# The state-space tables of a two-layer block, made in steps of four groups instead of two

## The chip, the cores and the metric

The kernel runs on one core of one Trainium2 chip. The metric is the device time of one execution in microseconds (us). Three runs of the kernel before gave 1955.3, 1954.03 and 1954.87 us, so the median is 1954.87 us. One execution was recorded by the profiler; its own time is 1953.94 us and its span, from the first to the last instruction, is 1951.7 us.

## The reference, cut to what matters

The reference is a two-layer block that works on 512 latent tokens and 256 context tokens of width 1024, in float32. Each layer normalises and modulates its input, projects it into four groups of heads (A: a gating MLP, B: a chunked linear attention, C: the state-space mixer S5, D: latent attention), joins them by an output projection, and then runs a gated MLP with a short convolution over its rows.

What the change touches is a part of group C. In the reference it reads:

```python
lam_bar = jnp.exp(lam * dt)
b_bar = ((lam_bar - 1.0) / lam)[..., None] * b
...
bu = jnp.einsum('bngi,gpi->bngp', u.astype(jnp.complex64), b_bar)
a = jnp.broadcast_to(lam_bar, bu.shape)
a_cum, h = lax.associative_scan(_linear_recurrence, (a, bu), axis=1)
...
ys_x.append(f(jnp.einsum('bngp,gop->bngo', hx, cmat).real))
```

There are 16 groups of 16 channels, 64 complex states in each, and two directions (the second runs over the flipped sequence).

## The kernel before, in words

**How the scan is tiled.** The kernel does not scan token by token. It cuts the sequence into chunks of 8 tokens. For each layer and each direction it prepares four tables from the parameters alone: `E` (how the 8 tokens of a chunk enter the state), `G` (how the state at a chunk's start reaches its 8 outputs), `K` (how tokens of one chunk reach one another) and `L` (the powers of lambda over whole chunks). The function `s5_tables` (from L446) makes them and stores them to DRAM; `mixer_c` (from L642) loads them and uses them.

**What a table step does.** After a prefix (exponentials, sine and cosine, powers of lambda up to 8, L453 to L530) and a set-up for each direction (L564 to L588), the groups are worked off in steps of two, so there are 8 steps in a direction and 16 in a layer. One step has six VectorE (DVE) operations: L600 and L601 multiply, L602 adds (128 x 288 elements each, the tile `gt`), and L623, L624, L625 do the same for the tile `et` (128 x 256 each). SyncE (SP) stores `gt` as `G` (L606). TensorE (PE) makes two small matmuls for `K` (L610) and two transposes of `et` (L627), all of them into one PSUM bank `kp`: columns 0 to 127 take the `K` part and columns 128 to 383 the transposes. ScalarE (ACT) copies the transposes to `es` (L629, 128 x 256), from where SP stores them as `E` (L630), and copies 64 rows of the `K` part to `ks` (L632). After the last step of a direction, `ks` is corrected (L634 or L636) and stored in four DMAs (L639).

**Buffers.** `gt`, `gt2` (the second product) and `et` have two buffers each, `es` and `ks` one. The PSUM tag is `pb1` in the first layer and `pn` in the second; both have two banks. The ten small tiles of the prefix (`are`, `aim`, `ldt`, `dt`, `mag`, `zr`, `zi`, `kk`, `sn`, `cs`) have a place of their own.

**When the steps are issued.** `s5_tables` is a generator, and a `yield` stands ahead of each step. For the first layer the prefix is traced at the start of the program; all the rest is traced at the beginning of `mixers`, after the opening stage, in which x is normalised and modulated (`nsa` L310, `nu` L388, `hh` L389, `hl` L390; the reciprocal root is taken on DVE in a chain of tiny operations, L132 to L138) and the first projection runs (`pm`). For the second layer it is traced inside the up-projection of the first layer's MLP: each call of `ffn_up` with c == 0 is followed by four `next(tables)`. One such call makes two products of 24 matmuls for 512 columns and 24 for 256 (`pf`, L198 to L200); their PSUM tiles are freed by ACT (L1196) and by DVE (L1198), which apply the convolution, and the weights are split into two parts by ACT (`whi`, L190) and DVE (`wlo`, L191).

**What sets the order.** The framework fixes the order of the instructions of each engine when the program is built. It simulates the program, prefers what was traced earlier, and lets later work fill the gaps that it foresees. At run time each engine works its queue off in that order: an instruction that waits holds back all that stands behind it on its engine. SP issues every DMA of the kernel, in order as well.

Of the kernel before, what the change touches and what calls it, by code (L numbers as in the profile page):

```python
# [15 lines left out]
ALU = mybir.AluOpType  # L16
# [73 lines left out]
class Net:  # L90
# [352 lines left out]
    def s5_tables(self, l, p, psp, p1):  # L443


        nc, tc = self.nc, self.tc  # L446
        tt, ts, stt = nc.vector.tensor_tensor, nc.vector.tensor_scalar, nc.vector.scalar_tensor_tensor
        n = 32

        def tl(tag, shape=(128, n)):  # L450
            return self.t(p, shape, tag)

        are, aim, ldt = tl("are"), tl("aim"), tl("ldt")  # L453
        self.load_sm(l, "are", are[:])
        self.load_sm(l, "aim", aim[:])
        self.load_sm(l, "ldt", ldt[:])
        dt, mag, zr, zi = tl("dt"), tl("mag"), tl("zr"), tl("zi")
# [4 lines left out]
        kk, sn, cs = tl("kk"), tl("sn"), tl("cs")  # L462
        ts(kk[:], zi[:], 0.15915494309189535, 12582912.0, op0=ALU.mult, op1=ALU.add)
# [16 lines left out]
        for d in range(2):  # L480
# [5 lines left out]
            m = 1  # L486
# [13 lines left out]

        fr, fi, dn, t1 = tl("ek"), tl("er"), tl("eq"), tl("kk")
        nr = tl("zr")
        for d in range(2):
# [15 lines left out]
        ev = self.s5d[l]  # L519
# [8 lines left out]

        early = [ld(x, 1, y) for x, y in (("bre", "bx"), ("bim", "by"), ("cx", "cx"), ("cy", "cy"))]
        yield  # L530

        cp = self.t(p, [128, 2, 128], "es", bufs=1)[:].rearrange("p r (m g) -> p r m g", m=8)
        for gh in range(2):
# [27 lines left out]
        for d in (1, 0):  # L561
# [5 lines left out]
            nc.vector.tensor_copy(eb[hi], pw[hi, 0, d])  # L567
            bre, bim, cx, cy = early if d else [ld(x, 0, y) for x, y in (
                ("bre", "bx"), ("bim", "by"), ("cx", "cx"), ("cy", "cy"))]
# [3 lines left out]
            b1 = self.t(p, [128, 2, 9, 16], "gt2", bufs=2)[:].rearrange("p a b c -> p (a b c)")[:, :256].rearrange(  # L573
                "p (a b) -> p a b", b=16)
# [13 lines left out]
            nc.vector.tensor_copy(bb[hi, :256], bbi[hi].rearrange("p a b -> p (a b)"))  # L588
            for g0 in range(0, 16, 2):
                yield  # L590
                gs = slice(g0, g0 + 2)

                sh = [128, 2, 9, 16]
                gt = self.t(p, sh, "gt", bufs=2)
                g2 = self.t(p, sh, "gt2", bufs=2)

                def co(c):
                    return c[:, :, gs].rearrange("p j g -> p g j").unsqueeze(3).to_broadcast(sh)

                tt(gt[:], cx[:, gs, :].unsqueeze(2).to_broadcast(sh), co(ea), op=ALU.mult)  # L600
                tt(g2[:], cy[:, gs, :].unsqueeze(2).to_broadcast(sh), co(eb), op=ALU.mult)  # L601
                tt(gt[:], gt[:], g2[:], op=ALU.add)  # L602
                jo, ko = 1 - d, d
                kp = self.t(psp, [128, 512], p1)[:]
                pe = kp[:, 128:384]
                nc.sync.dma_start(ev["G"][:, d, gs, :],  # L606
                                  gt[:, :, jo:jo + 8, :].rearrange("p g j o -> p g (j o)"))
                for g in range(g0, g0 + 2):
                    q = g % 4
                    nc.tensor.matmul(kp[32 * q:32 * q + 32, 0:128],  # L610
                                     bb[:, g * 16:g * 16 + 32],
                                     gt[:, g - g0, ko:ko + 8, :].rearrange("p j o -> p (j o)"),
                                     start=True, stop=True)

                sh2 = [128, 2, 8, 16]
                et = self.t(p, sh2, "et", bufs=2)
                e2 = self.t(p, sh, "gt2", bufs=2)[:].rearrange("p a b c -> p (a b c)")[:, :256].rearrange(
                    "p (g s i) -> p g s i", g=2, s=8)
# [674 lines left out]
    def run(self, out):  # L1293
# [76 lines left out]
        for l in range(L):  # L1370
# [4 lines left out]
            with self.pool("f") as fp, self.pool("psf", space=PSUM) as psp:  # L1375
# [43 lines left out]
                with ExitStack() as ye:  # L1419
# [368 lines left out]
```

## Time and profile before

| what | value |
|---|---|
| median of three runs | 1954.87 us (1954.03 to 1955.3) |
| profiled execution, its own time | 1953.94 us |
| its span | 1951.7 us |
| PE busy | 1793.4 us (92%) |
| DVE busy | 1201.3 us (62%) |
| ACT busy | 784.5 us (40%) |
| mean granted TensorE clock | 0.931 of full speed |
| chain that ended last: PE, DVE, issue, ACT | 68%, 15%, 10%, 4% |

"Busy" is the time in which an engine has at least one instruction running. The chain that ended last is followed back from the last instruction, at each step to what released it. Idle time of an engine that is not on that chain costs nothing. The duration of a DVE row is longer than the distance to the next row, because neighbours overlap a little; the distance from start to start is what a queue full of work pays.

### The profile page before, as it was taken

What the parts mean: (1) busy time and instruction counts of PE and PEld (TensorE: products, weight loads), DVE (VectorE), ACT (ScalarE), POOL (GpSimd) and SP (SyncE); (2) the same over time, 40 slices, a digit from 0 to 9 for tenths busy, and PEclk for the clock granted to TensorE, in tenths of its full rate; (3) what the DMA queues carried; (4) which work ended last, traced back from release to release, by engine and by line L of the source; (5) the groups of instructions that cost most, each with busy time, mean ns of one, the idle gap of its engine ahead of it and who ended that gap; (6) DMA issues with size and microseconds to landing.
All of it is one profiled execution on the core that took longest, in us unless ns stands there. A gap on an engine that the chain in (4) does not pass through costs nothing.

```text
span 1951.7 us, 28485 instructions
## 1 busy us (share of the span) xinstructions
PE 1793.4 (92%) x11256; PEld 1535.1 (79%) x11256; DVE 1201.3 (62%) x2296; ACT 784.5 (40%) x1284; POOL 124.1 (6%) x142
## 2 busy tenths in 40 slices
PE   5799999789989899999999987997979999999997
PEld 2577687569987688888888886986668988888886
DVE  8938644555788963674575575684465666364646
ACT  3332744245763333332331354355434554343432
POOL 0000000000340000000000034000000130000002
PEclk7699998779999999999999987998788989999998
DMA  9374621002633333443344243322100722323241
GB/s 352 99 253 168 209 85 42 28 25 101 216 110 107 112 106 108 124 138 117 123 130 136 66 146 105 115 75 86 42 23 23 238 78 84 109 86 108 87 132 63
DMA packets 96949, 222.18 MB, mean 114 GB/s; under 512 B 11440, under 2 KB 45616, under 8 KB 95792
## 3 DMA queue, kind: packets, MB, share of 16 engines
q1 hardware_dynamic: 96816, 220.36, 35.3%
q8 instruction: 89, 1.46, 0.3%
q14 instruction: 44, 0.36, 0.1%
HBM read 193.35 MB, written 24.08 MB: 111 GB/s over the span
## 4 chain that ended last, share of the span: by engine, by line
PE 68%; DVE 15%; issue 10%; ACT 4%; DMA 2%; POOL 1%; SPq 1%; POOLq 0%; DVEq 0%; ACTq 0%
PE pf L198 15%; PE pf L199 15%; PE pf L200 15%; PE pg L198 3%; PE pg L200 3%; PE pg L199 3%; DVE wlo L191 1%; PE pd L1142 1%; DVE z L1198 1%; PE pb L242 1%; DVE nu L388 1%; PE pn L321 1%; PE pc L767 1%; DVE junk L235 1%; DVE hlx L390 1%
## 5 line engine op out<-in xcount | busy, mean ns | idle before, releaser
L191 DVE TENSOR_TENSOR wlo<-raw,whi 128x1024 fp32r<-128x1024 f32 (+1 forms) x215 | 252.4, 1174 | 306.4 <-ACT whi L190 303.4
L190 ACT ACTIVATE whi<-raw 128x1024 fp32r<-128x1024 f32 (+1 forms) x215 | 217.4, 1011 | 403.0 <-PE pf L199 326.7
L198 PE MATMUL pf<-hhx,whi 128*128 128x512 f32 (+1 forms) x1032 | 364.8, 359 | 15.1 <-DVE z L1198 8.8
L199 PE MATMUL pf<-hlx,whi 128*128 128x512 f32 (+1 forms) x1032 | 367.9, 358 | 6.1 <-DVE hlx L390 5.9
L200 PE MATMUL pf<-hhx,wlo 128*128 128x512 f32 (+1 forms) x1032 | 366.5, 356 | 2.0 <-DVE wlo L191 1.8
L198 PEld LDWEIGHTS pf<-hhx,whi 128*128 128x128 f32 x1032 | 198.7, 195 | 43.4 <-ACT hhx L389 5.6
L199 PEld LDWEIGHTS pf<-hlx,whi 128*128 128x128 f32 x1032 | 201.0, 195 | 33.5 <-DVE hlx L390 8.8
L200 PEld LDWEIGHTS pf<-hhx,wlo 128*128 128x128 f32 x1032 | 200.9, 195 | 28.8 <-DVE wlo L191 3.0
L198 PE MATMUL pf<-g,whi 128*128 128x512 f32 (+1 forms) x552 | 185.0, 341 | 5.8 <-DVE z L1198 3.1
L200 PE MATMUL pf<-g,wlo 128*128 128x512 f32 (+1 forms) x552 | 186.4, 340 | 0.8 <-DVE wlo L191 0.8
L199 PE MATMUL pf<-g,whi 128*128 128x512 f32 (+1 forms) x552 | 186.9, 340 | 0.0
L1198 DVE SCALAR_TENSOR_TENSOR z<-pf,cols,z 128x511 f32<-128x511 f32 (+1 forms) x264 | 168.3, 655 | 24.2 <-ACT z L1196 21.8
L199 PE MATMUL pf<-hl,whi 128*128 128x256 f32 x432 | 123.5, 287 | 0.5 <-DVE hl L390 0.5
L198 PE MATMUL pf<-hh,whi 128*128 128x256 f32 x432 | 122.0, 287 | 1.6 <-ACT hh L389 1.5
L200 PE MATMUL pf<-hh,wlo 128*128 128x256 f32 x432 | 122.6, 285 | 0.0
L198 PEld LDWEIGHTS pf<-g,whi 128*128 128x128 f32 x552 | 104.2, 191 | 19.2 <-issue 3.9
L200 PEld LDWEIGHTS pf<-g,wlo 128*128 128x128 f32 x552 | 105.2, 191 | 12.3 <-DVE wlo L191 1.0
L199 PEld LDWEIGHTS pf<-g,whi 128*128 128x128 f32 x552 | 105.3, 191 | 11.6 <-DVE g L1248 0.2
L1196 ACT ACTIVATE z<-pf,cols 128x512 f32<-128x512 f32 (+1 forms) x132 | 90.0, 696 | 33.9 <-PE pf L200 29.3
L1277 DVE TENSOR_TENSOR y<-y,pf 128x512 f32<-128x512 f32 (+1 forms) x88 | 44.2, 513 | 72.4 <-PE pf L200 72.3
L124 POOL TENSOR_TENSOR nroy<-nroy,mhalf 128x2 f32<-128x2 f32 x10 | 10.0, 996 | 1232.4 <-DVE nroy L123 900.7
L198 PEld LDWEIGHTS pf<-hh,whi 128*128 128x128 f32 x432 | 83.0, 194 | 3.7 <-ACT hh L389 2.1
(467 smaller groups left out, 3489.4 us busy)
## 6 DMA issues: line engine op xcount, KB each, us to landing
raw<-in_w SPq DMA_DIRECT2D x170, 512.0 KB, 3.5
rawm<-in_wmod SPq DMA_DIRECT2D x64, 512.0 KB, 4.2
raw<-in_w SPq DMA_DIRECT2D x48, 384.0 KB, 3.1
wm<-in_wmod SPq DMA_DIRECT2D x8, 1024.0 KB, 11.1
silu<-in_wmod SPq DMA_DIRECT2D x16, 512.0 KB, 5.5
dx<-g SPq DMA_DIRECT2D x32, 256.0 KB, 2.2
dG<-gt SPq DMA_DIRECT2D x32, 128.0 KB, 1.9
dE<-es SPq DMA_DIRECT2D x32, 128.0 KB, 1.8
```

What stands on the lines that cost most here:

```text
L190: nc.scalar.activation(hv, src, AF.Copy)
L191: nc.vector.tensor_tensor(lv, src, hv.bitcast(F32), op=ALU.subtract)
L198: self.nc.tensor.matmul(out, lh, rh, start=i == 0, stop=False)
L199: self.nc.tensor.matmul(out, lh, rl, start=False, stop=False)
L200: self.nc.tensor.matmul(out, ll, rh, start=False, stop=i == n - 1)
L235: self.nc.vector.scalar_tensor_tensor(junk[:], wt, 1.0, self.silu[w][:], op0=ALU.mult, op1=ALU.mult, accum_out=self.modacc[l][:, w, m:m + 1])
L242: self.nc.tensor.matmul(acc[32 * q:32 * q + 2, :], self.ct[:, k, :], halves[q // 2][:, q % 2 * 512:q % 2 * 512 + 512], start=k == 0, stop= ...
L321: self.nc.tensor.matmul(ps[:, j:j + 1], acc[:, k, j * 128:(j + 1) * 128], self.ones[:, 0:1], start=k == 0, stop=k == 1)
L388: nc.vector.scalar_tensor_tensor(u[:], xk, sc, pb, op0=ALU.mult, op1=ALU.mult)
L1196: nc.scalar.activation(z[:, o:o + m], p[:, :m], AF.Identity, bias=b, scale=w1)
L1198: self.last = nc.vector.scalar_tensor_tensor(z[:, o + d:o + d + m - 1], p[:, s:s + m - 1], w, z[:, o + d:o + d + m - 1], op0=ALU.mult, op1 ...
L1277: nc.vector.tensor_tensor(y[:, m, t0:t0 + tw], y[:, m, t0:t0 + tw], ps[:, :tw], op=ALU.add)
```

## The change

The groups of a direction are worked off in four steps of four groups. Each of the six DVE operations of a step is twice as wide (128 x 576 and 128 x 512 elements). One PSUM bank `kp` is taken at the first step of a direction and holds the `K` parts of all four steps; `ks` is copied from it once, after the last step. The four transposes of a step go into another bank `pe`, taken at each step. `gt` keeps two buffers of double size; `gt2` and `et` have one buffer of double size each, `es` stays at one, of double size. The ten small tiles of the prefix are moved into the tile that is later used for `ks`. In the up-projection each `ffn_up` call with c == 0 is followed by two `next(tables)` instead of four. There are now 10 pieces of the generator instead of 18: the first call takes the prefix and the first set-up, the next four calls take two steps each (with the second set-up in the third call). Before, the first call took two steps of two groups as well, the next three calls had four each, and the fifth had the last two.

```diff
+        def four(tag, j=9):
+            return self.t(p, [128, 4, 9, 16], tag, bufs=2 if tag == "gt" else 1)[:, :, :j]
+        early = tl("ks", (128, 4, 128))[:].rearrange("p a b -> p (a b)")
+        small = {}
+        def sm(tag):
+            return small.setdefault(tag, early[:, len(small) * n:len(small) * n + n])
...
-            for g0 in range(0, 16, 2):
+            kp = None
+            for g0 in range(0, 16, 4):
                 yield
-                gs = slice(g0, g0 + 2)
-                sh = [128, 2, 9, 16]
-                gt = self.t(p, sh, "gt", bufs=2)
-                g2 = self.t(p, sh, "gt2", bufs=2)
+                if kp is None:
+                    kp = self.t(psp, [128, 512], p1)
+                gs = slice(g0, g0 + 4)
+                sh = [128, 4, 9, 16]
+                gt, g2 = four("gt"), four("gt2")
...
-                kp = self.t(psp, [128, 512], p1)[:]
-                pe = kp[:, 128:384]
...
-                for g in range(g0, g0 + 2):
-                    q = g % 4
-                    nc.tensor.matmul(kp[32 * q:32 * q + 32, 0:128],
+                for q in range(4):
+                    nc.tensor.matmul(kp[32 * q:32 * q + 32, g0 * 32:g0 * 32 + 128],
...
-                et = self.t(p, sh2, "et", bufs=2)
+                et = self.t(p, sh2, "et", bufs=1)
+                e2 = four("gt2", 8)
...
+                pe = self.t(psp, [128, 512], p1)
-                for g in range(2):
+                for g in range(4):
                     nc.tensor.transpose(pe[:, g * 128:g * 128 + 128], ...)
-                es = self.t(p, [128, 2, 128], "es", bufs=1)
-                nc.scalar.copy(es[:].rearrange("p g c -> p (g c)"), pe)
-                nc.sync.dma_start(ev["E"][:, d, g0:g0 + 2, :], es[:])
-                rs = slice(g0 % 4 * 32, g0 % 4 * 32 + 64)
-                nc.scalar.copy(ks[rs, g0 // 4, :], kp[rs, 0:128])
+                es = self.t(p, [128, 4, 128], "es", bufs=1)
+                nc.scalar.copy(es[:].rearrange("p g c -> p (g c)"), pe[:])
+                nc.sync.dma_start(ev["E"][:, d, gs, :], es[:])
+            nc.scalar.copy(ks[:].rearrange("p a b -> p (a b)"), kp[:])
...
                             if c == 0:
-                                for _ in range(4):
+                                for _ in range(2):
                                     next(tables, None)
```

## Rows read from the trace of the kernel before

**Rows 1.** The page, the span in 40 slices of 48.8 us, tenths busy.
```profile
PE   5799999789989899999999987997979999999997
DVE  8938644555788963674575575684465666364646
```

**Rows 2.** Stretches: busy us of each engine (instructions), granted clock, DMA share, GB/s.
```profile
48.00:62.00 14.00, 10.45 (x69) 7.07 (x68) 14.00 (x47) 5.64 (x17) 0.00 (x0) 0.80 0.51 175
62.00:77.00 15.00, 9.80 (x38) 6.98 (x38) 14.70 (x51) 5.02 (x12) 0.88 (x2) 0.50 0.27 77
...
98.00:110.00 12.00, 10.11 (x56) 7.36 (x53) 4.43 (x9) 6.51 (x14) 0.00 (x0) 0.86 0.73 256
...
632.00:658.00 26.00, 21.08 (x128) 16.76 (x127) 25.31 (x62) 9.14 (x18) 0.00 (x0) 1.00 0.47 139
701.00:720.00 19.00, 17.98 (x99) 15.51 (x98) 11.36 (x18) 8.14 (x12) 0.00 (x0) 1.00 0.37 117
```

**Rows 3.** DVE's instructions in order, 47 to 62 us: start, duration, line, tiles.
```profile
48.73 0.16 DVE L133 TENSOR_SCALAR nri<-nrx 128x2 int32<-128x2 int32 x1
...
53.07 0.15 DVE L137 TENSOR_TENSOR nrt<-nrt,nri 128x2 f32<-128x2 f32 x1
53.14 0.41 DVE L625 TENSOR_TENSOR et<-et,gt 128x256 f32<-128x256 f32 x1
53.48 0.42 DVE L623 TENSOR_TENSOR et<-bbr,ea 128x256 f32<-128x256 f32 x1
53.81 0.45 DVE L602 TENSOR_TENSOR gt<-gt,gt 128x288 f32<-128x288 f32 x1
54.18 0.15 DVE L138 SCALAR_TENSOR_TENSOR nry<-nrt,nri 128x2 f32<-128x2 f32 x1
...
59.97 0.15 DVE L138 SCALAR_TENSOR_TENSOR nry<-nrt,nry 128x2 f32<-128x2 f32 x1
```

**Rows 4.** DVE's instructions in order, for distances from start to start.
```profile
23.73 0.44 DVE L600 TENSOR_TENSOR gt<-cx,ea 128x288 f32<-128x288 f32 x1
24.10 0.41 DVE L623 TENSOR_TENSOR et<-bbr,ea 128x256 f32<-128x256 f32 x1
24.43 0.44 DVE L601 TENSOR_TENSOR gt<-cy,eb 128x288 f32<-128x288 f32 x1
...
27.98 0.67 DVE L310 TENSOR_TENSOR nsa<-nsa,nsq 128x512 f32<-128x512 f32 x1
28.58 0.41 DVE L623 TENSOR_TENSOR et<-bbr,ea 128x256 f32<-128x256 f32 x1
...
81.62 0.42 DVE L623 TENSOR_TENSOR et<-bbr,ea 128x256 f32<-128x256 f32 x1 [0.94 <-PE pb L627]
82.08 0.42 DVE L625 TENSOR_TENSOR et<-et,gt 128x256 f32<-128x256 f32 x1
```

**Rows 5.** ACT's instructions in order: the copies, and one wait.
```profile
97.41 0.37 ACT L629 COPY es<-pb 128x256 f32<-128x256 f32 x1 [3.04 <-PE pb L627]
97.81 0.26 ACT L632 COPY ks<-pb 64x128 f32<-64x128 f32 x1
...
101.95 0.58 ACT L676 COPY s5a<-pc 96x512 f32<-96x512 f32 x1 [1.18 <-PE pc L675]
...
696.42 1.06 ACT L190 ACTIVATE whi<-raw 128x1024 fp32r<-128x1024 f32 x1 [7.40 <-PE pf L199]
...
697.84 0.36 ACT L629 COPY es<-pn 128x256 f32<-128x256 f32 x1
```

**Rows 6.** Who waited for whom, 0 to 110, then 590 to 700: total us, times, longest.
```profile
ACT es L629 <- DMA dE<-es: 12.0, 6, 3.9
...
ACT es L629 <- DMA dE<-es: 11.1, 6, 2.4
PE pf L198 <- DVE z L1198: 8.8, 5, 2.5
DVE et L623 <- PE pn L627: 3.4, 1, 3.4
```

More of the change, by code (lines that the diff above doesn't have):

```diff
@@ L451, in tl @@
             return self.t(p, shape, tag)
-        are, aim, ldt = tl("are"), tl("aim"), tl("ldt")
+        def four(tag, j=9):
[4 more added lines that the diff above has]
+            return small.setdefault(tag, early[:, len(small) * n:len(small) * n + n])
+        are, aim, ldt = sm("are"), sm("aim"), sm("ldt")
         self.load_sm(l, "are", are[:])
@@ L499, in s5_tables @@
                 m *= 2
-        fr, fi, dn, t1 = tl("ek"), tl("er"), tl("eq"), tl("kk")
-        nr = tl("zr")
+        fr, fi, dn, t1 = tl("ek"), tl("er"), tl("eq"), sm("kk")
+        nr = sm("zr")
         for d in range(2):
@@ L527, in ld @@
             return dst
-        early = [ld(x, 1, y) for x, y in (("bre", "bx"), ("bim", "by"), ("cx", "cx"), ("cy", "cy"))]
+        first = [ld(x, 1, y) for x, y in (("bre", "bx"), ("bim", "by"), ("cx", "cx"), ("cy", "cy"))]
         yield
-        cp = self.t(p, [128, 2, 128], "es", bufs=1)[:].rearrange("p r (m g) -> p r m g", m=8)
+        cp = self.t(p, [128, 4, 128], "es", bufs=1)[:, :2].rearrange("p r (m g) -> p r m g", m=8)
         for gh in range(2):
@@ L567, in s5_tables @@
             nc.vector.tensor_copy(eb[hi], pw[hi, 0, d])
-            bre, bim, cx, cy = early if d else [ld(x, 0, y) for x, y in (
+            bre, bim, cx, cy = first if d else [ld(x, 0, y) for x, y in (
                 ("bre", "bx"), ("bim", "by"), ("cx", "cx"), ("cy", "cy"))]
@@ L572, in s5_tables @@
             fib = fi[:, d * 16:d * 16 + 16].unsqueeze(2).to_broadcast([128, 16, 16])
-            b1 = self.t(p, [128, 2, 9, 16], "gt2", bufs=2)[:].rearrange("p a b c -> p (a b c)")[:, :256].rearrange(
+            b1 = self.t(p, [128, 4, 9, 16], "gt2", bufs=1)[:].rearrange("p a b c -> p (a b c)")[:, :256].rearrange(
                 "p (a b) -> p a b", b=16)
@@ L597, in co @@
                 def co(c):
                     return c[:, :, gs].rearrange("p j g -> p g j").unsqueeze(3).to_broadcast(sh)
-                tt(gt[:], cx[:, gs, :].unsqueeze(2).to_broadcast(sh), co(ea), op=ALU.mult)
-                tt(g2[:], cy[:, gs, :].unsqueeze(2).to_broadcast(sh), co(eb), op=ALU.mult)
-                tt(gt[:], gt[:], g2[:], op=ALU.add)
+                tt(gt, cx[:, gs, :].unsqueeze(2).to_broadcast(sh), co(ea), op=ALU.mult)
+                tt(g2, cy[:, gs, :].unsqueeze(2).to_broadcast(sh), co(eb), op=ALU.mult)
@@ L603, in s5_tables @@
+                tt(gt, gt, g2, op=ALU.add)
                 jo, ko = 1 - d, d
-                kp = self.t(psp, [128, 512], p1)[:]
-                pe = kp[:, 128:384]
                 nc.sync.dma_start(ev["G"][:, d, gs, :],
                                   gt[:, :, jo:jo + 8, :].rearrange("p g j o -> p g (j o)"))
-                for g in range(g0, g0 + 2):
-                    q = g % 4
-                    nc.tensor.matmul(kp[32 * q:32 * q + 32, 0:128],
-                                     bb[:, g * 16:g * 16 + 32],
-                                     gt[:, g - g0, ko:ko + 8, :].rearrange("p j o -> p (j o)"),
+                for q in range(4):
+                    nc.tensor.matmul(kp[32 * q:32 * q + 32, g0 * 32:g0 * 32 + 128],
+                                     bb[:, (g0 + q) * 16:(g0 + q) * 16 + 32],
+                                     gt[:, q, ko:ko + 8, :].rearrange("p j o -> p (j o)"),
@@ L613, in s5_tables @@
                                      start=True, stop=True)
-                sh2 = [128, 2, 8, 16]
-                et = self.t(p, sh2, "et", bufs=2)
-                e2 = self.t(p, sh, "gt2", bufs=2)[:].rearrange("p a b c -> p (a b c)")[:, :256].rearrange(
-                    "p (g s i) -> p g s i", g=2, s=8)
+                sh2 = [128, 4, 8, 16]
+                et = self.t(p, sh2, "et", bufs=1)
+                e2 = four("gt2", 8)
                 def ce(c):
```

4 lines of the change are left out of this document (2 added, 2 removed).

## The prediction, made before the change was run

> **What bounds the kernel now.** I went from the slices to the stretches, then to single instructions. In the slices PE is busy nine tenths or more nearly everywhere, and where it is not, DVE is high [rows 1]. The two dips that concern us are the first two slices (PE 5 and 7, DVE 8 and 9) and the slices around 590 to 690 us (DVE 8 and 9 again). These are the two places where the state-space tables are made. A change to the tables can move the end only there, or through what they hand on.
>
> The stretches say how tight it is [rows 2]. From 48 to 62 us DVE is busy 14.00 of 14 us, from 62 to 77 us 14.70 of 15, while PE has 10.45 and 9.80 us of work at a granted clock of 0.80 and 0.50, so part of the time it was at its 1.2 GHz level. After 98 us DVE falls to 4.43 of 12 us and PE takes over. In the second layer's tables one call of the up-projection (632 to 658 us) has DVE at 25.31 of 26 us. The call from 701 to 720 us has DVE at 11.36 of 19 and PE at 17.98 of 19: there PE is the bound, and DVE work is free.
>
> Why DVE decides, and not only by its total, is seen in its order of instructions [rows 3]. The reciprocal root for the second token group is a chain of two-element operations, the second of them at 48.73, the last at 59.97 us. Between two neighbours of that chain, 53.07 and 54.18, three table operations stand in the queue. The chain waits for no one; it goes slowly because table work is queued between its links. So the tables lie on the opening path although the opening needs none of them.
>
> **The change, part by part.**
>
> *DVE operations.* Distances from start to start count, since the queue is full [rows 4]: 0.37 us for 128 x 288 (23.73 to 24.10), 0.33 for 128 x 256 (24.10 to 24.43), 0.60 for 128 x 512 (27.98 to 28.58). For 128 x 576 I extrapolate: 0.60 + 64 x (0.60 - 0.37)/224 = 0.67 us, an estimate. Two old steps cost 6 x 0.37 + 6 x 0.33 = 4.20 us; a new one 3 x 0.67 + 3 x 0.60 = 3.81. That saves 0.4 us for each of 8 new steps in a layer, 3.2 us a layer, 6.4 in all.
>
> Here a rule of the Trainium skill would give more. The rows show the next operation starting 0.37 us after one whose own duration is 0.44 [rows 4]. The page "VectorE: DVE Perf Modes", section "The DRAIN you can't avoid", says that the next op does not start until the pipe has emptied, which would make the duration the price: 12 durations of 0.44 and 0.41 against 6 of 0.74 and 0.67 save 0.88 us a step, 14 us in all instead of 6.4. The trace disagrees with that rule as it stands there (the same page allows that an op which is not held starts earlier), and I go by the distances.
>
> *Lost interleaving.* `gt2` and `et` go from two buffers to one. Now the operations of two steps can stand alternately; afterwards `gt2` forces second product, sum, next second product, sum to follow one another. An operation right behind its own producer started 0.46 us after it instead of 0.33 (81.62 to 82.08) [rows 4]: 0.13 us for each such pair. Three pairs in a step would cost 0.39 x 8 = 3.1 us a layer, none costs 0. I take one in a step, since the first product of the next step and the free `et` product can stand between: 1.0 us. Net for DVE: -2.2 us a layer, between -3.2 and -0.1.
>
> *What of it is on the path.* In the first layer DVE is full from 48 us to the end of the opening, so I count all of -2.2. In the second layer the five calls alternate between a full DVE and a full PE [rows 2], so I count -1.5 of -2.2 (ends: 0 and -3.2).
>
> *The step that moves.* With two pieces a call instead of four, four groups (3.8 us of DVE) go from the first call to the fifth, which is bounded by PE and has 7.6 us of DVE time free. The ends are 0 and -3.8. Since the planner pulls table work forward into gaps anyway, the place of the `next` decides little; I take -0.8.
>
> *ACT.* Old: 16 x (0.37 + 0.26) = 10.1 us a layer for the copies of `es` and `ks`. New: 8 + 2 copies of 512 columns at 0.58 (the row of 96 x 512) = 5.8 us [rows 5]. The 4.3 us saved lie on an engine that is idle more than half of the time (5.64 of 14, 9.14 of 26) [rows 2], so they are worth nothing by themselves. But `es` has one buffer, and its copy waited 12.0 and 11.1 us in the two stages for the store of the copy before [rows 6], holding back whatever stood behind it on ACT, the weight splits and the convolution's first pass among it. Eight copies instead of sixteen, one every 3.8 us or more of DVE work, meet that wait seldom. I take -0.5 (ends 0 and -2).
>
> *PE, SP, prefix.* PE makes the same 64 small matmuls and 32 transposes a layer; nothing. SP issues 8 stores fewer of `G` and of `E` each per layer, and none is on the path that I can show; nothing, at most a gain for the loads behind them. `ks` is copied once at the end instead of bit by bit, so the last four stores of a direction come one 0.58 us copy later, where PE has other work (10.11 of 12 us after 98 us) [rows 2]. The small tiles share a place with `ks`, whose next writer is DVE too: nothing.
>
> *Sum.* -2.2 (first layer) - 1.5 (second) - 0.8 (moved step) - 0.5 (ACT) = -5.0 us. The profiled execution took 1953.94 us, 2.2 us more than its span, and becomes 1948.9; the median of the runs is 0.93 us higher, so 1949.9 us. The favourable ends together give -3.2 - 3.2 - 3.8 - 2 = -12.2 us, which is 1942.7; the unfavourable ones leave nothing.
>
> **The rivals.**
>
> *The path loses the tables (faster by more).* With one buffer of `gt2` and `et`, fewer table operations are ready at a time. If the planner then puts one long operation between two links of the root's chain instead of two or three short ones, each link shrinks from about 1.1 to 0.7 us. With nine links from 48.73 to 59.97 that is 3.6 us more, and the same holds for the convolution's passes in the second layer. The work left out goes to where PE is the bound. Against it: nothing in the rows says how the order will come out. Time: 1943.
>
> *The long operations fill as much (no change).* If two of them stand between two links, that is 1.27 us instead of 1.04, 0.23 x 9 = 2 us more in this chain and about as much in the chain for the third token group behind it. From -5.0 some -1 is left: 1953.9 us, no difference.
>
> *The single buffers stall PE and DVE (slower).* A step's transposes now need the one free PSUM bank, so they wait for the `es` copy of the step before, and the next `et` product waits for the transposes. That copy stands in ACT's queue behind a weight split, which once waited 7.40 us for PE itself [rows 5]. With two half-size buffers, DVE already waited once 3.4 us for PE to finish its transposes, and PE waited up to 2.5 us for DVE [rows 6]. It decides from where a step's copy ends later than the next step's `et` sum, 3.8 us of DVE work on. If 3 or 4 of the 16 new steps are caught for 2.5 to 3.4 us, that costs about 10 us and leaves +5: 1960 us. What is queued behind the waiting transposes is the whole up-projection. For it: PE works its queue in order and has no slack there. Against it: there are half as many meeting points, and ACT is seldom behind by that much. The Trainium skill has the rule that speaks for this rival: "Double-buffer for performance", on the page "Trainium Kernel Development and Optimization", section "Best Practices". The row of 3.4 us agrees that a buffer can run out here; how often with one buffer no row of before can show.
>
> **How the numbers follow.** Forecast 0.45 (its own range 1946 to 1952.5), larger gain 0.12, no change 0.23, slower 0.20. A measurement of this kernel tells 0.2% (3.9 us) from no change, so faster means below 1951.0 and slower above 1958.8. Of the forecast 0.36 lies below 1951.0; with the larger gain that is 0.48. The rest of the forecast and nearly all of the third case make 0.31, the last case and a tail of the third 0.21. The range from 1942 to 1959 leaves out about half of the largest gains and half of the stalls, 0.16 together.
>
> **What would show it.** Right: table operations of DVE at distances of 0.60 and 0.67 us; DVE busy time lower by some 5 us over the two stages; the waits of `es` for its own store down from 23 us to a few; the last matmul of the opening projection 2 us earlier; calls of the up-projection around 600 to 700 us shorter by 2 to 3 us together, with more DVE work in the fifth. Wrong: waits of PE for `es` or of DVE for transposes that add up to more than 5 us; a root's chain longer than the 11.2 us of now; or a gain that lies outside 0 to 110 and 580 to 720 us, which none of my steps would explain.

## The result

The changed kernel took 1929.91 us in the median (1923.23 to 1937.35 us, four runs) against 1954.77 us for the kernel before (1954.03 to 1955.3, four runs): a ratio of 0.9874 with a 95% interval of 0.9832 to 0.9916. In a second series it was 0.9873 (0.9858 to 0.9888). The gain is 25 us; the forecast was 5, and the lower end of its range 1942. The profiled execution took 1925.66 us, its span is 1923.6 us.

From the page of the changed kernel, the span in 40 slices, tenths busy and tenths of the full clock [rows 1]:

```profile
PE   4799999789989899999999988997988999999997
DVE  8938544555789952764675585684564675454645
PEclk8799998689999999999999986997998999999998
```

The clock row of the kernel before, which the prediction did not use:

```profile
PEclk7699998779999999999999987998788989999998
```

The tables are made in the first two slices and in the 13th to 15th. Both rows also dip around the eighth slice and from the 24th on, where the mixers and the latent attentions of the two layers stand, and they differ there as well. The prediction did not look at these slices.

Stretches of the changed kernel that answer to the two full ones in the opening and to two calls of the up-projection [rows 2], each shifted by what had been gained by then:

```profile
45.00:59.00 14.00, 11.24 (x76) 10.35 (x76) 13.48 (x36) 6.05 (x12) 0.00 (x0) 0.74 0.76 255
59.00:74.00 15.00, 9.45 (x37) 7.48 (x34) 14.75 (x45) 4.61 (x10) 0.85 (x2) 0.50 0.19 63
...
620.00:646.00 26.00, 22.30 (x130) 18.66 (x129) 25.75 (x48) 9.80 (x15) 0.00 (x0) 0.93 0.50 146
...
683.00:702.00 19.00, 17.93 (x96) 15.26 (x97) 12.09 (x19) 7.39 (x12) 0.00 (x0) 1.00 0.40 115
```

DVE is nearly as full as before where it was full (13.48 us for 14.00, 14.75 for 14.70, 25.75 for 25.31), with fewer instructions (36 for 47, 45 for 51, 48 for 62). DVE's order in the root's chain of the changed kernel [rows 3 and 4]:

```profile
49.72 0.16 DVE L133 TENSOR_SCALAR nri<-nrx 128x2 int32<-128x2 int32 x1
...
54.01 0.15 DVE L138 SCALAR_TENSOR_TENSOR nry<-nrt,nri 128x2 f32<-128x2 f32 x1
54.08 0.75 DVE L615 TENSOR_TENSOR gt<-gt,gt 128x576 f32<-128x576 f32 x1
54.74 0.15 DVE L136 SCALAR_TENSOR_TENSOR nrt<-nrx,nry 128x2 f32<-128x2 f32 x1
54.86 0.69 DVE L633 TENSOR_TENSOR gt<-bbi,eb 128x512 f32<-128x512 f32 x1
55.47 0.15 DVE L137 TENSOR_TENSOR nrt<-nrt,nry 128x2 f32<-128x2 f32 x1
...
59.94 0.15 DVE L138 SCALAR_TENSOR_TENSOR nry<-nrt,nry 128x2 f32<-128x2 f32 x1
```

The chain takes 10.2 us from its second link to its last instead of 11.2: in the lines shown one long operation stands between two links now; elsewhere in the chain there are up to two. Who waited for whom in the changed kernel, 0 to 110 us, then 575 to 715 us [rows 6]:

```profile
ACT es L639 <- PE pb L637: 11.9, 4, 3.7
PE pb L637 <- ACT es L639: 2.7, 1, 2.7
ACT es L639 <- DMA dE<-es: 0.8, 1, 0.8
...
PE pf L198 <- DVE z L1207: 3.8, 5, 2.1
...
DVE et L632 <- PE pn L637: 3.1, 1, 3.1
PE pn L637 <- DVE et L634: 3.0, 1, 3.0
...
ACT es L639 <- DMA dE<-es: 2.4, 1, 2.4
PE pn L637 <- DVE ks L645: 2.1, 1, 2.1
```

The waits of `es` for its own store fell from 23.1 to 3.2 us, as forecast. In the opening its copy waited longer for the transposes instead (11.9 us for 6.1 before).

**Where the time went.** I took every matmul that both kernels have and subtracted its start in the first profile of the kernel before; the table gives how much this shift grew within each stage (us, medians over neighbouring matmuls). The stages are cut at 140, 330, 400, 505, 715, 1375 and 1500 us of the kernel before: opening; first layer's mixers; start of its latent attention; rest of that attention; up-projection with the second layer's tables; all up to the second layer's mixers; the end of those with the second attention. "Half" is the time in a whole profile at the lower clock level (273 us in the first profile of the kernel before).

| kernel | opening | mixers | start | attention 1 | tables 2 | up to 1375 | attention 2 | half | median |
|---|---|---|---|---|---|---|---|---|---|
| before_again | 0.1 | 0.7 | -0.1 | -0.1 | 0.2 | 0.4 | 2.8 | 290 | 1957.9 |
| changed kernel | -2.9 | -1.7 | 0.0 | -6.4 | -6.4 | -2.5 | -9.2 | 246 | 1929.9 |
| after_again | -3.4 | -1.7 | 0.0 | -6.0 | -7.0 | -0.4 | -0.5 | 263 | 1931.2 |
| l0_new | -4.5 | -1.0 | 0.0 | -6.5 | 2.8 | -2.6 | -4.3 | 256 | 1941.5 |
| l1_new | 0.2 | 4.0 | -0.7 | -0.6 | -0.5 | -1.5 | 3.0 | 290 | 1957.0 |
| banks_only | 0.2 | 2.3 | -3.1 | -6.7 | 4.0 | -0.8 | 3.1 | 288 | 1953.5 |
| four_two_banks | -3.4 | 0.6 | -3.2 | -0.4 | -3.9 | 0.3 | 2.9 | 280 | 1943.6 |
| after_attention_old_order | -4.0 | -1.7 | 0.1 | -0.1 | -6.5 | -3.1 | 6.7 | 277 | 1946.2 |
| before_attention_new_order | -0.4 | 4.0 | -2.8 | -2.5 | 2.2 | 0.2 | -3.8 | 285 | 1954.1 |
| two_single_buffers | -7.9 | 2.4 | -8.1 | -0.1 | 0.1 | -0.2 | -4.1 | 263 | 1932.3 |
| after_four_nexts | -4.6 | 0.6 | 0.0 | -5.7 | -5.8 | -1.5 | 6.0 | 261 | 1941.0 |
| after_scores_ahead | -1.3 | -0.6 | 0.7 | -0.4 | -6.7 | -0.6 | -0.5 | 271 | 1943.7 |
| before_three_orders | 0.2 | 0.8 | -14.1 | -2.3 | -0.3 | -3.3 | -4.2 | 242 | 1934.1 |
| single_buffers_new_order | -8.9 | 4.3 | -1.1 | -2.2 | -2.5 | 0.3 | -0.2 | 278 | 1944.3 |
| both_gains | -8.2 | 4.0 | -10.0 | -1.5 | 2.5 | -1.8 | -3.4 | 249 | 1936.0 |
| after_third_order | -4.9 | -0.8 | -9.9 | -5.8 | -6.0 | 0.8 | -3.5 | 244 | 1930.2 |
| three_orders_new_l1_tables | 0.9 | 3.7 | -1.8 | -2.5 | -4.7 | -5.4 | -9.0 | 249 | 1928.9 |

In the three kernels with single buffers in the first layer the matmuls around 140 us stand in another order, so there only the sum of opening and mixers is safe.

Of the changed kernel's 29 us in that profile only 9.3 lie in the two table stages; 6.4 and 9.2 lie in the attentions, where nothing was edited. The last two columns go together over the kernels. In both pairs of profiles (273 and 246 us, 290 and 263 us) the changed kernel was 27 us less at the lower level than the kernel before. A matmul is shown below to take 1.9 times as long at that level, so this is worth at most 13 us (an estimate; TensorE waits for part of that time): up to half of the gain can have come by way of the clock.

### The profile page after: what moved, and what is told of

It reads as the page before. It is cut to its first block, busy times and chain, and to the rows that moved or that the text cites. A ratio compares the mean times of both kernels' runs of the same rounds, so it can differ in the third digit from the quotient of the medians.

```text
span 1923.6 us, 28254 instructions
## 1 busy us (share of the span) xinstructions
PE 1776.5 (92%) x11256; PEld 1527.7 (79%) x11256; DVE 1193.7 (62%) x2200; ACT 775.7 (40%) x1240; POOL 122.3 (6%) x142
## 4 chain that ended last, share of the span: by engine, by line
PE 69%; DVE 14%; issue 9%; ACT 4%; DMA 2%; POOL 1%; SPq 0%; POOLq 0%; DVEq 0%; ACTq 0%
PE pf L198 16%; PE pf L199 16%; PE pf L200 16%; PE pg L198 3%; PE pg L200 3%; PE pg L199 3%; PE pd L1151 1%; DVE z L1207 1%; DVE wlo L191 1%; PE pb L242 1%; DVE nu L388 1%; PE pc L776 1%; DMA bx<-in_sm 1%; PE pn L321 1%; DVE hlx L390 1%
## 5 line engine op out<-in xcount | busy, mean ns | idle before, releaser
L200 PEld LDWEIGHTS pf<-g,wlo 128*128 128x128 f32 x552 | 104.6, 190 | 12.4 <-DVE wlo L191 1.0
L199 PEld LDWEIGHTS pf<-hl,whi 128*128 128x128 f32 x432 | 83.5, 193 | 3.6 <-DVE hl L390 2.2
```

Of the source, the lines that this page charges most:

```text
L199: self.nc.tensor.matmul(out, lh, rl, start=False, stop=False)
L200: self.nc.tensor.matmul(out, ll, rh, start=False, stop=i == n - 1)
```

## The experiments

**Which half of the change, and which layer.** l0_new and l1_new take the new tables in one layer alone. banks_only keeps steps of two and takes only the new use of the PSUM banks. four_two_banks makes steps of four but copies the `K` part after every step from a bank taken at every step.

```diff
 l0_new:  tables = self.s5_tables_two(1, ...)   # layer 0 new, layer 1 old
 l1_new:  tables = self.s5_tables_two(0, ...)   # layer 0 old, layer 1 new
 banks_only:
+                if kp is None:
+                    kp = self.t(psp, [128, 512], p1)
+                pe = self.t(psp, [128, 512], p1)[:, :256]
 four_two_banks:
-            nc.scalar.copy(ks[:].rearrange("p a b -> p (a b)"), kp[:])
+                nc.scalar.copy(ks[:, g0 // 4, :], kp[:, :128])
```

> Layer 0 makes its tables the new way, layer 1 the old way (four pieces a call). Theory A (the gain outside the table stages comes from another order of PE's work in attention, which the planner gives after the new layer-0 tables; this kernel has the order of after in both attentions): the opening and the first mixers gain 3 to 5 us, attention of layer 0 gains 6, the tables of layer 1 gain 0, attention of layer 1 gains 10; in all -17 to -22, near 1935. Theory B (the whole gain is cheaper table work, and what shows up in attention is the clock, which differs from run to run): -3 to -5 us, near 1950, with attention as in before.

> Layer 0 makes its tables the old way, layer 1 the new way (two pieces a call). The planned order in the attention of layer 0 is that of before, in layer 1 nearly so. Theory A: opening 0, attention of layer 0 gains 0, the tables of layer 1 gain 6, attention of layer 1 gains 0 to 2; near 1948. Theory B (clock by luck): attention moves by as much as in after in some of the runs although the order is that of before, so 1935 to 1948 with a wide spread.

> Steps of two groups and four pieces a call as in before, all SBUF buffers as in before; only the PSUM part is changed: the K matmuls of a direction in one bank with one copy to ks at its end, the transposes in another bank. The planned order in the attention of layer 0 is exactly that of after, in layer 1 nearly that of before. Theory A: attention of layer 0 gains 6 us, attention of layer 1 0 to 2, the two table stages 0 to 2 together (16 copies of ks fewer a layer, same DVE work); near 1947. Rival (wide steps bring everything): within 2 us of before, 1953 to 1956.

> Steps of four groups and two pieces a call as in after, but the K part of each step goes into a PSUM bank of that step and is copied to ks in each step, so kp and pe alternate. The planned order in both attentions is nearly that of before. Theory A: opening and layer-1 tables gain 7 to 10 us as in after, both attentions gain nothing; near 1946. Rival (the single bank for a direction is what frees the table stages): the table stages gain less than 4 us. Rival B (clock by luck): attention gains as in after although the order is that of before.

Measured: 0.9932 (0.9909 to 0.9955), 1.0009 (0.9999 to 1.0019), 0.999 (0.9977 to 1.0004) and 0.9948 (0.9936 to 0.996) of the kernel before. None of the parts has the gain, and l0_new and l1_new don't add up to it. Only four_two_banks (1943.6 us) came out near theory A. l0_new (1941.5) fell between its two theories, l1_new (1957.0) missed both, and the time of banks_only (1953.5) is that of its rival: what it gained at the start of the first attention and in it (9.8 us) it lost in the mixers, the second layer's tables and the second attention (9.4). The stages say more: the kernels fall into two classes in the first attention. Those in which the planner chose another order of matmuls there (the changed kernel, l0_new, and banks_only, which has no wide operation) gained 6.0 to 6.7 us; those with the old order 0.4 to 0.6. So the gain in that stage goes with the order and not with the width of the steps, and the new use of the banks is enough to bring it about. Why the planner's simulation turns over there I did not find.

**What the order is worth.** TensorE's matmuls outside the tables are traced in the same order in both kernels, so the planned order of one can be forced on the other by edges that bind only the issue order (192 and 370 pairs in the two attentions). They bind TensorE alone: the orders of ACT and DVE are planned anew.

```diff
+        for a, b in zip(seq, seq[1:]):
+            tc.add_manual_dep(ins[b].ins, ins[a].ins.name, mybir.DependencyInfo(mybir.DependencyClass.NoSync, mybir.DependencyReason.DATA), reason="order")
```

> The changed kernel itself, a second time, so that its times and its stages can be compared with the other kernels of the same series. In the profiled run its gain over the kernel before lay at four places: the opening -2.9 us, the latent attention of the first layer -6.4, the tables of the second layer -6.4, the mixers and the attention of the second layer -10.4. If these are properties of the program, the second profile shows each of them again within 2 us, and the median is 1925 to 1935. If part of it is chance of the granted clock (the four runs so far go from 1923 to 1937), the second layer's attention falls back to between -2 and -6, and the median is above 1935.

> The changed kernel, with TensorE's order in the latent attention of both layers forced to that of the kernel before (191 and 369 neighbouring pairs of matmuls are tied by ordering edges; tables, buffers and banks are those of the changed kernel). Theory A (the order of the matmuls in attention, which the planner chose anew, carries the larger part of the gain): the attention of the first layer gives back 4 us, that of the second 7, the median is 1940 to 1943. Rival B (the order there is worth nothing, the gain comes from elsewhere and from the granted clock): within 3 us of the changed kernel.

> The kernel before, with TensorE's order in the latent attention of both layers forced to that of the changed kernel (ordering edges; the tables are made in steps of two groups as before). Theory A: -4 us in the first attention and -7 in the second, 1943 to 1947. Rival B: 1953 to 1957, as the kernel before.

> The kernel before once more, for a second profile of it: which stages repeat from run to run. By theory A the attention of the first layer and that of the second take as long as in the first profile within 2 us. By rival B (chance of the granted clock) some stage of it differs by 4 us or more from the first profile, and the stages of the first profile that looked slow are not the same.

The second profile of the changed kernel repeats the first within 0.7 us up to 715 us; in the second attention it falls back from -9.2 to -0.5. The old order takes 15 us from the changed kernel (0.9955, 0.9937 to 0.9972), 6 of them in the first attention and 7 in the second against after_again. The new order on the kernel before gave only 2.3 us (0.9995, 0.9981 to 1.0008), so theory A missed there and the time is that of rival B: 9.1 us were gained at three places, and 4.0 in the first mixers and 2.2 in the tables were lost in that profile. The 4.0 are the clock: from 140 us to the end of the mixers all three engines work in the order of the kernel before, at a granted clock of 0.95 instead of 0.98.

What the order does is seen in TensorE's rows. The kernel before, where the idle time stands in brackets with what ended it:

```profile
426.89 0.28 PE L200 MATMUL pd<-hh,pl 96*128 96x256 f32 x1
430.59 0.90 PE L1135 MATMUL pe<-cst,pr 128*128 128x128 f32 x3 [3.42 <-ACT pr L1129]
...
439.54 0.90 PE L1135 MATMUL pe<-cst,pr 128*128 128x128 f32 x3 [2.51 <-ACT pr L1129]
```

The same place in after_again:

```profile
421.77 0.28 PE L200 MATMUL pd<-hh,pl 96*128 96x256 f32 x1
424.31 0.58 PE L198 MATMUL pe<-hh,pq 96*128 96x256 f32 x1 [2.26 <-ACT df L1171]
...
426.40 0.84 PE L1144 MATMUL pe<-cst,pr 128*128 128x128 f32 x3
```

Before, the transposes of the first tile's probabilities stood right behind its scores, and TensorE waited for ACT's exponentials, twice: 5.9 us. In the new order the nine score matmuls of another tile stand between, and the transposes find `pr` ready. Instead those scores wait 2.26 us for ACT's copy `df`, which reads the PSUM tile that they take. Over the whole stage TensorE's waits fell from 10.9 to 7.5 us; the rest of the 6 us goes with the clock (granted 0.91 before, 0.96 in after_again).

before_attention_new_order has the same order of matmuls in this stage, but gained only 2.5 us there, and the four other kernels with these forced orders and steps of two in the first layer 1.5 to 2.5. ACT there is not in the changed kernel's order. In before_attention_new_order the exponentials stand ahead of that copy, as in the kernel before:

```profile
430.38 0.90 ACT L1130 ACTIVATE pr<-pd,dmx 128x768 f32<-128x768 f32 x1 [2.15 <-DVE dmx L1128]
431.27 0.36 ACT L1163 COPY df<-pe 128x256 f32<-128x256 f32 x1
```

In after_again they stand behind it:

```profile
423.89 0.37 ACT L1171 COPY df<-pe 128x256 f32<-128x256 f32 x1 [1.61 <-DVE hlx L1195]
424.75 0.90 ACT L1138 ACTIVATE pr<-pd,dmx 128x768 f32<-128x768 f32 x1 [0.49 <-DVE dmx L1136]
```

So the scores wait 3.7 us for the copy, in all five kernels. In before_attention_new_order products wait 1.6 us more for `pt`, and over the stage TensorE waits 10.1 us, hardly less than in the kernel before. Forcing TensorE alone does not carry over the whole order.

In the second attention the waits shift. Waits of TensorE at 1396 to 1471 us in before_again:

```profile
PE pd L198 <- DVE hlx L1062: 6.3, 2, 5.5
PE pd L1142 <- DVE hlx L1137: 2.4, 2, 1.3
```

And at 1377 to 1452 us in after_again, the same two:

```profile
PE pd L198 <- DVE hlx L1071: 2.2, 1, 2.2
PE pd L1151 <- DVE hlx L1146: 0.7, 1, 0.7
```

Over the whole stage the fall is smaller, 14.2 to 12.3 us, since after_again waits longer for exponentials there. after_attention_old_order waits 19.5 us in it, at about the clock of the two (0.79; 0.79 in before_again, 0.77 in after_again). That is the 7 us against after_again, but also 5 us more than before_again has with the same order of TensorE (4.2 us for `bon` instead of 0.5, 6.1 for exponentials instead of 2.8). So about 5 of the 15 us may be the price of mixing one engine's old order with the others' new one.

**What the clock does to it.** Both executions of the changed kernel have the same instructions in the same order, yet the second attention differs by 8.7 us. The profiled run of the result:

```profile
1374.69 1.99 PE L1086 MATMUL pd<-wg,ck 96*128 96x256 f32 x8
...
1390.03 2.82 PE L1098 MATMUL pd<-ck,wg 96*64 96x512 f32 x4
```

The profiled run of after_again:

```profile
1376.29 3.78 PE L1086 MATMUL pd<-wg,ck 96*128 96x256 f32 x8
...
1397.50 2.82 PE L1098 MATMUL pd<-ck,wg 96*64 96x512 f32 x4
```

The same eight matmuls take 1.99 us at 2.4 GHz and 3.78 at 1.2 GHz, and the stretch between the two rows is 21.2 us long instead of 15.3. After_again reached it 1.6 us later; whether that is why its clock fell there no run shows. The four runs of the result differ in the same way: 1923.2 and 1925.7 us at a mean granted clock of 0.935 and 0.937, 1934.2 and 1937.4 us at 0.931 and 0.930. So their spread goes with the clock and is no property of the change.

**The forecast's own terms, each alone.** Single buffers of `gt2` and `et` in steps of two; four calls of `next` as before; and, as a test of the theory, scores traced one tile ahead.

```diff
 two_single_buffers:    g2 = self.t(p, sh, "gt2", bufs=1); et = self.t(p, sh2, "et", bufs=1)
 after_four_nexts:      for _ in range(4): next(tables, None)
 after_scores_ahead:
+                if qt + 1 < nq:
+                    ps = scores(h, qt + 1)
+                attend(h, qt, now)
```

> The kernel before (steps of two groups) with one buffer each of gt2 and et instead of two: the price of the single buffers by itself. The planner gives it the old order in the attention of the first layer and the new one in that of the second. The forecast's term (an operation right behind its producer starts 0.13 us later, no stalls): the two table stages change by 0 to +3 us each, the first attention by 0, the second by -1 to -5 as in the other kernels with the new order there: 1951 to 1958. The rival of stalls (the transposes and the et products wait for one another): +5 or more in each table stage, with waits of DVE for PE at et above 8 us in a stage, 1960 to 1968.

> The changed kernel with four calls of next after each up-projection call instead of two: the step that moved, by itself. The forecast's term (0.8 us, ends 0 and 3.8): the table stage of the second layer is 0 to 2 us longer than the -6 us that the changed kernel shows there, the rest the same, 1930 to 1935. Rival (the place of the step carries the larger part of the gain in that stage): 4 us or more are lost there, 1935 to 1938.

> The changed kernel, with the scores of the next query tile traced ahead of the softmax of the one before, so that the planner prefers what the new order did by chance in one place. If the waits of TensorE for the exponentials are what the order of the attention is worth (theory A), the attention of both layers gets no longer, and may lose the 4 to 6 us of waits for df and hlx that are left: 1925 to 1931. Rival: there are two PSUM tiles for scores; held by scores that are made early, they hold back the projections of the next head, and the attention gets 2 to 6 us longer: 1933 to 1940.

two_single_buffers contradicted both expectations: 1932.25 us, 0.9868 (0.9846 to 0.9891), the whole gain of the change from taking two buffers away. The stalls are there. Its waits from 580 to 715 us:

```profile
ACT es L629 <- PE pn L627: 21.4, 6, 5.7
DVE et L623 <- PE pn L627: 14.1, 5, 4.0
```

But that stage was no longer than in the kernel before (+0.1), and the planner, with other buffers to foresee, arranged the opening (-7.9) and the start of the first attention (-8.1) anew. after_four_nexts gave 0.9917 (0.9892 to 0.9943), 1941.0 us, slower than both its expectations. The tables of the second layer were 0.6 to 1.2 us worse than with two calls, as the forecast had it, but the two profiles of the changed kernel differ by 0.6 us there themselves. 6.5 us went in the second attention (against after_again), where TensorE's order is nearly that of the kernel before.

after_scores_ahead was 12.6 us slower than after_again, 0.9934 (0.9916 to 0.9951), slower than both its expectations as well, and it does not test what it was made for. In the first attention its TensorE has the order of the kernel before, transposes right behind their own scores, and the two waits are back:

```profile
429.38 0.90 PE L1152 MATMUL pe<-cst,pr 128*128 128x128 f32 x3 [3.41 <-ACT pr L1146]
438.05 0.90 PE L1152 MATMUL pe<-cst,pr 128*128 128x128 f32 x3 [2.66 <-ACT pr L1146]
```

The planner did not put the scores where they were traced. The run is one more kernel with new tables and TensorE's old order in that attention, which gained 0.4 us; whether scores further ahead would gain stays open.

**Order alone, and sums.** The order at the start of the first attention, taken from two_single_buffers, was forced as well: first on the kernel before with its own tables, then the new attention orders on single buffers, and on a mixture (single buffers in the first layer, steps of four in the second).

> The kernel before, tables and buffers untouched, with TensorE's order forced in three places: the start of the first layer's latent attention as in the kernel with single buffers (its query projection stands ahead of the last products of the linear attention), the attention of both layers as in the changed kernel. Theory A (order alone): -8 us at the first place, -6 and -4 at the other two, less some 3 us that the tables of the second layer gave back whenever the first attention was shorter: 1942 to 1948. Rival (the order helps only together with the tables that led to it, as the kernel with two forced places, 1954.1, seems to say): 1951 to 1956.

> Steps of two groups with one buffer each of gt2 and et, with TensorE's order in the attention of both layers forced to that of the changed kernel. Theory A: another -6 us in the first attention on top of the 1932.3 of that kernel, 1924 to 1930, so below the changed kernel without one wide operation. Rival (orders of different origin don't add up, since the clock gives it back): 1931 to 1936.

> Tables of the first layer in steps of two with single buffers (opening -7.9 us, start of the first attention -8.1), those of the second in steps of four (-6), TensorE's order in the attention of both layers forced to that of the changed kernel (-6 and -4). Theory A, the sum of the stages less 4 us for the second layer's tables, which gain less where the order around them differs: 1918 to 1928. Rival as for the kernel above: 1931 to 1940.

before_three_orders took 1934.06 us, 0.9886 (0.9873 to 0.9898): 21.7 us without one edit to the tables, more than expected. The start of the first attention in the kernel before:

```profile
345.30 2.85 PE L1101 MATMUL pd<-cq,dwq 128*128 128x512 f32 x8
353.19 1.54 PE L949 MATMUL pb<-cst,bon 128*128 128x128 f32 x6 [5.03 <-DVE bon L936]
355.01 2.82 PE L1089 MATMUL pd<-ck,wg 96*64 96x512 f32 x4 [0.28 <-ACT df L1106]
...
359.71 4.79 PE L1101 MATMUL pd<-cq,dwq 128*128 128x512 f32 x8 [0.41 <-DVE hl L1092]
```

In before_three_orders (all of TensorE's rows outside the tables pass through one recording line there, so go by the tiles):

```profile
349.15 1.50 PE L1794 MATMUL pd<-ck,wg 96*64 96x512 f32 x4 [0.55 <-ACT df L1107]
353.90 4.53 PE L1794 MATMUL pd<-cq,dwq 128*128 128x512 f32 x8 [3.25 <-DVE hl L1093]
358.67 0.88 PE L1794 MATMUL pb<-cst,bon 128*128 128x128 f32 x6 [0.24 <-DVE bon L937]
```

The products that wait for `bon` now stand behind the second head's projections. But TensorE's waits in the whole stretch (335 to 405 us, here to 392) only fell from 14.4 to 12.4 us; most of the 14.1 us is the clock. Two stretches of the kernel before (the granted clock is the third number from the right):

```profile
355.00:370.00 15.00, 11.86 (x31) 5.72 (x31) 7.63 (x10) 3.65 (x5) 0.00 (x0) 0.71 0.26 87
...
385.00:400.00 15.00, 12.81 (x50) 9.96 (x51) 4.38 (x12) 4.04 (x10) 0.00 (x0) 0.58 0.01 2
```

And of before_three_orders:

```profile
355.00:370.00 15.00, 11.23 (x61) 7.53 (x60) 10.90 (x21) 4.47 (x8) 0.00 (x0) 0.92 0.20 70
370.00:385.00 15.00, 11.79 (x86) 10.86 (x85) 5.79 (x14) 4.85 (x11) 0.00 (x0) 0.89 0.05 19
```

single_buffers_new_order has the same order at this place and gained only 1.1 there. Its stretches from 360 us:

```profile
360.00:375.00 15.00, 13.24 (x52) 10.56 (x51) 5.32 (x10) 3.76 (x8) 0.00 (x0) 0.50 0.18 61
375.00:390.00 15.00, 13.29 (x62) 12.54 (x61) 3.50 (x9) 2.78 (x7) 0.00 (x0) 0.50 0.01 2
```

It was at 1.2 GHz in the whole of both and came to 1944.31 us, 0.9941 (0.9923 to 0.9958), 12 us slower than two_single_buffers, from which it differs by the forced orders alone; both_gains came to 1935.97, 0.9902 (0.9886 to 0.9918). In both, theory A's sum missed; both_gains fell in its rival's range, single_buffers_new_order beyond it.

three_orders_new_l1_tables, which follows below, shows the clock by itself. Up to this place all three engines work in the order of before_three_orders, yet it gained 1.8 us here and not 14.1:

```profile
360.00:375.00 15.00, 12.36 (x45) 8.85 (x44) 10.06 (x17) 4.46 (x8) 0.00 (x0) 0.61 0.23 81
375.00:390.00 15.00, 13.07 (x59) 11.75 (x57) 3.69 (x8) 2.93 (x6) 0.00 (x0) 0.50 0.02 7
```

The six kernels with this order gained 1.1, 1.8, 8.1, 9.9, 10.0 and 14.1 us at this place: what the same order gives differs with the clock, and gains of order from different kernels don't add up.

The last two ask what the tables give when the attention's order is held.

> The changed kernel, with TensorE's order at the start of the first layer's attention forced as in before_three_orders (the query projection ahead of the last products of the linear attention); the order of both attentions is held as the changed kernel has it. If tables and order add up: the tables' own part (-3 in the opening, -6 in the second layer) and this order's 8 to 14 us give 1918 to 1926, faster than both kernels. If the granted clock takes it back, as in single_buffers_new_order, where the stretch from 358 us stayed at half clock for 38 us: 1928 to 1936.

> before_three_orders (1934.1) with the second layer's tables in steps of four groups: the tables' part alone, with TensorE's order in attention held equal. If the wide steps gain by themselves what the second layer's stage showed in the changed kernel: -6 us, 1926 to 1930. If only what the forecast counted for that stage (1.5 to 2.8 us): 1931 to 1933. If they gain nothing there, as in the kernel with the new tables in the second layer alone: 1933 to 1937.

after_third_order took 1930.16 us, 0.9865 (0.984 to 0.9891); three_orders_new_l1_tables 1928.94, 0.9848 (0.9826 to 0.987). Against before_three_orders, with the same three orders, the tables of both layers gave 3.9 us and those of the second alone 5.1 (4 and 7 us by the ratios to the kernel before of the same series); the intervals overlap in the first case and just part in the second. after_third_order fell in the range of its second expectation, where the clock takes the gain back, three_orders_new_l1_tables in that of its first. Neither is measurably faster than the changed kernel.

## Why the prediction was right or wrong

**Wrong: "A change to the tables can move the end only there, or through what they hand on."** This step failed. The planner orders the whole program in one simulation, so other tables gave other orders in the attentions hundreds of microseconds later. No term and no rival had a price for that; the text had only named it as what no step would explain. The two table stages hold 9.3 and 10.4 us of the gain in two profiles, twice the forecast, and most of the rest lies in the two attentions. With TensorE's old order forced on both attentions the changed kernel gives back 15 of its 25 us.

The 25 us can't be split cleanly between tables, order and clock. With TensorE's order in the attentions held, the changed tables are worth 10 us on the old order (after_attention_old_order), 23 on the changed kernel's order (1954.1 us of before_attention_new_order to 1931.2 of after_again) and 4 where three places are forced (before_three_orders to after_third_order). The forced kernels hold one engine of three, and the clock differs between them. How much is which stays open.

**Right: the price of the wide operations.** 0.66 us from start to start for 128 x 576 (54.08 to 54.74) and 0.61 for 128 x 512 (54.86 to 55.47), against 0.67 and 0.60 in the forecast. The rule of the Trainium skill ("VectorE: DVE Perf Modes", "The DRAIN you can't avoid") by which the next operation waits until the pipe has emptied does not fit these rows either: their durations are 0.75 and 0.69. The page lets an operation that is not held start earlier, so these rows may fall under that exception; no run compares held operations with others.

**Right in the opening, too small in the second layer.** The opening gained 2.9 and 3.4 us in the two profiles, and between 1.3 and 4.9 in all eight profiles of kernels with the new tables there, against 2.2 plus a part of ACT's 0.5. The second layer's tables gained 6.4 and 7.0 against 1.5 + 0.8 and the rest of ACT's 0.5. The moved step (0.8 in the forecast, 0.6 to 1.2 measured) is as small as was said, but no larger than the difference of two profiles. No run prices lost interleaving or ACT's part alone. TensorE's waits for `z`, which stands behind the tables on DVE, fell from 8.8 [rows 6] to 3.8 us, which the forecast did not count by itself. It stays open how much of this stage is width, how much the order within it and how much the clock: new tables there gained 3.9 to 7.0 us in seven profiles, but -0.5, +2.5 and -4.7 in the three that have them in the second layer alone (a minus is a gain; old tables there: -2.5 to +4.0).

**The rival of single buffers was wrong in its price.** Its waits exist: in the changed kernel DVE waited 3.1 and 0.6 us for transposes and TensorE 2.7 us for `es`. Their sum of 6.4 us passes the 5 that the prediction had named as a sign of being wrong. In two_single_buffers DVE waited 14.1 us in the second layer's tables, but the stage was as long as before (+0.1), though TensorE's waits for `z` rose from 8.8 to 10.8. So the stalls did not show in the time. The rule "Double-buffer for performance" (the Trainium skill, "Trainium Kernel Development and Optimization", "Best Practices") is given there for overlapping DMA with compute. No DMA moves `gt2` or `et`, so it bears less on this rival than the prediction took it to, and these runs do not test it. The kernel with fewer buffers was faster by 1.3%, with other orders in opening and attention.

**The rival of the lost path had a right half.** The root's chain did get shorter, by 1.0 us where it had said 3.6.

## What to carry to other kernels

Where a planner orders the program, an edit's effect is its own price plus a new order of everything behind it; compare the planned orders of both programs first, on every engine. Ordering edges can hold an order while an edit is priced, but edges on one engine leave the others free: here they made 5 us of new waits in one kernel, and in another TensorE's waits hardly fell. TensorE's order around softmax and around late products is worth trying by itself: three forced stretches gave 21.7 us here, a good part of it by way of the clock. One profile cannot price a stage in which the clock varies; take two of the same program before a difference of less than 9 us is believed.

## What the runs showed of the hardware that was not expected

The granted clock differs between executions of one program: the changed kernel was 246 and 263 us at 1.2 GHz in two of them, and one stretch took 15.3 us in one and 21.2 in the other with the same instructions in the same order on all three engines. A matmul costs 1.9 times as much at the lower level (3.78 against 1.99 us). So a stage can gain more than the waits that were taken out of it (14.1 us at the start of the first attention, where the waits fell by 2.0), or next to nothing: with the same order the same stage gained 1.8 us in another kernel.
